# Order of filling products in the last attention's loop, and of the units ahead of it

## The chip, the cores and the metric

One core of a Trainium2 chip runs the whole program. The metric is the device time of one execution in microseconds; lower is better. TensorE (PE) multiplies matrices into PSUM, ScalarE (ACT) and VectorE (DVE) empty PSUM and do the pointwise work, GpSimd (POOL) and SyncE (SP) mostly issue transfers.

## The reference

Two blocks run one after the other on 512 tokens of width 1024. The first is a two-layer transformer; the second, which matters here, is one hybrid layer: a dilated window attention with three groups of heads beside a long convolution, merged by gates. Cut to the attention:

```python
for g, (window, dilation) in enumerate(((128, 1), (512, 4), (2048, 16))):
    radius = window // (2 * dilation)
    o_g, lse_g = dilated_window_attention(qkv[:, :, 0, g], qkv[:, :, 1, g],
                                          qkv[:, :, 2, g], slopes, dilation, radius)
    ...
wts = jax.nn.softmax(jnp.stack(lses, axis=0), axis=0)
o_attn = jnp.einsum('bgsh,gbshe->bshe', wts, jnp.stack(outs, axis=0))
y_attn = o_attn.reshape(B, S, D_ATTN) * jax.nn.silu(g_attn)
```

A softmax over the three groups' own softmaxes equals one softmax over the keys of all three, so the kernel handles each query's 512 + 128 + 128 = 768 scores at once. All is fp32; products of weights are made as three passes over high and low parts.

## The kernel before

**Planner.** The program is written against a scheduler that lays out each engine's instructions from the order in which the code emits them: among instructions whose inputs and buffers are ready in its own model of time, the one emitted first goes first. So the emitted order is a priority. Weight loads and splits stand under a raised priority (AHEAD, 1500 places), so they run ahead. On the chip every engine then takes its instructions strictly in the order laid out.

**Weights.** `unit` brings a block of 1024 x 256 weights in two halves: a transfer on SP into one of three `raw` buffers (L102), a copy to the high part on ACT (L276), the low part on DVE (L277). Two units fit in the weight buffers, so the halves of a further unit are split as the halves of an older one fall free.

**Products.** `mm3` (L282 to L284) issues three matmuls per 128 rows of depth, 24 per product. A queries/keys unit (`queries`, L1287 and on) gives two products of 512 columns, evicted by ACT with 128x512 each: first the queries (L1300, `qT`), then the keys (L1298, `kT`); six products make one pair of heads' three groups. A value unit (`values`) gives four products of 256 columns, evicted by DVE with the bias added (L1256, `v`). `b2_rattn` gives eight products evicted as sigmoids (L1384, `sr`). Each of these is a generator that yields after a product.

**Attention.** `b2_attn` runs four passes, one per pair of heads, with four tasks each (128 queries by 768 keys, for both heads b = 0 and 1). A task has these steps: `scores` (12 matmul instructions, L1338, into the only four-bank buffer `S`); `soft` (per head: DVE adds the distances and takes the extreme, L1346, writing `P`; ACT exponentiates with the sum, L1348; DVE takes the reciprocal, L538, and scales, L542); `prod`, which is `pv_two`: for each head two groups of three 128 x 128 turns (transposes, L516, six per head) into `ptr`, a copy of each group by ACT (L520, `PT`), and at every second task the products with the values (L530, L533) for both; and `after` the fourth task (L1362).

`ptr` and the products of the loop share one ring of three one-bank PSUM buffers (L1325). `P` has three buffers, two of which a task takes (L1345). `pipeline` (L564) emits the tasks one ahead of each other and calls `fill`, which draws a fixed number of products (`steps`, L1367) from the next pass's queries and values; every second of them also draws a step of `stage_weights` (two loads, a scaling on DVE L1227, a split, and two stores L1235), which prepares weights of a later stage. The mix stages call `pipeline` as well, without products to draw.

Ahead of the loop, `run(...)` makes two value units and the first pair's queries and keys with the PSUM pools of the stage before; they are closed at the first pass and the four banks of `S`, one of `ops` and three of the ring take their place.

Of the kernel before, what the change touches and what calls it, by code (L numbers as in the profile page):

```python
# [45 lines left out]
class Net:  # L46
# [138 lines left out]
    def fill(self, n=1):  # L185

        for _ in range(n):
            if self.fillers:
                self.begun = True
                if next(self.fillers[0], "end") == "end":  # L190
                    self.fillers.pop(0)
                    self.begun = False
# [371 lines left out]
    def pipeline(self, tasks, depth, beside=iter(()), steps=(), deep=None):  # L564

        n = len(tasks)  # L570
        ahead = depth

        def fill(m):
            for _ in range(steps[m] if m < len(steps) else 0):
                next(beside, None)
        for t in tasks[:depth]:
            t[0]()
        tasks[0][1]()
        fill(0)
        for m, t in enumerate(tasks):  # L580
            while ahead < n and ahead <= m + (depth if deep is None or m + 1 < deep else depth + 1):
                tasks[ahead][0]()
                ahead += 1
            if m + 1 < n:
                tasks[m + 1][1]()
            t[2]()
            if t[3] is not None:
                t[3]()
            fill(m + 1)
        for _ in beside:  # L590
            pass

# [645 lines left out]
    def b2_attn(self):  # L1238
        nc, tc, a = self.nc, self.tc, self.a
        mm = nc.tensor.matmul  # L1240
        with ExitStack() as es, ExitStack() as rs:
# [4 lines left out]
            def val_bias(g, s):  # L1246
                bv = ap.tile([128, 256], F32, name="bv", tag="bv", bufs=2)
                nc.gpsimd.dma_start(bv, a["b_v_2"][:, 512 * g + 256 * s:512 * g + 256 * s + 256].to_broadcast([128, 256]))
                vals[s].append(ap.tile([128, 4, 256], F32, name="v", tag="v", bufs=4))
                return bv  # L1250

            def value(W, bv, t, s):
                p = self.product()
                for k in range(KB):
                    self.mm3(p[:, :256], [x[:, k, 128 * t:128 * t + 128] for x in self.h2], W[k], k == 0, k == KB - 1)
                nc.vector.tensor_tensor(vals[s][-1][:, t], p[:, :256], bv, OP.add)  # L1256
# [23 lines left out]
            def values(s, g):  # L1280
                W = self.b2_units(2 + 9 * s + g)
                bv = val_bias(g, s)
                for t in range(4):
                    value(W, bv, t, s)
                    yield

            def queries(p_):  # L1287
                qT = ap.tile([128, 3, 512], F32, name="qT", tag="qT", bufs=2)
                kT = ap.tile([128, 3, 512], F32, name="kT", tag="kT", bufs=2)
                qk.append((qT, kT))  # L1290
                for g in range(3):
                    W = self.b2_units(5 + 9 * (p_ // 2) + 3 * (p_ % 2) + g)
                    for b in range(2):
                        p = self.product()
                        for k in range(KB):
                            self.mm3(p, [w[:, 128 * b:128 * b + 128] for w in W[k]], [x[:, k] for x in self.h2], k == 0, k == KB - 1)
                        if b:
                            nc.scalar.activation(kT[:, g], p, AF.Identity, bias=self.bias2(12 + 4 * g + p_))  # L1298
                        else:
                            nc.scalar.activation(qT[:, g], p, AF.Identity, bias=bq[:, g, p_:p_ + 1], scale=scq[:, p_:p_ + 1])  # L1300
                        yield

            def run(*work):
                for _ in chain(*work):
                    pass
# [5 lines left out]
                        next(stage, None)  # L1311
                    yield
            qk, sr = [], []
            run(values(0, 1), values(0, 2), queries(0))
            for s in range(2):
                for pp in range(2):
                    p_ = 2 * s + pp
# [552 lines left out]
```

## Time and profile before

| | |
|---|---|
| Median of 3 runs | 3403.52 us (3399.89 to 3403.88) |
| Profiled execution | 3408.37 us, its span 3406.6 us |
| TensorE busy | 3339.2 us, 98% of the span |
| DVE, ACT, POOL busy | 58%, 32%, 10% |
| Granted TensorE clock, mean | 0.994 |
| Chain that ended last | PE 85%, DVE 5%, issue 5%, DMA 3% |

The span runs from the first to the last instruction of the profiled execution; the rest of its time lies around it. Busy shares are of the span. A matmul's end is modelled: the next one starts well before the end shown (512 columns: 0.39 us shown, 0.23 us from start to start), so rates are read from starts. "Idle before" in a row is the time for which the engine had nothing running, with the instruction that ended the wait.

### The profile page before, as it was taken

To read this page: it belongs to the slowest core of one execution; us is meant where nothing else is said; L and a number is where in the kernel's file an instruction comes from. 1 tells how busy PE (TensorE), PEld (TensorE's weight loads), DVE (VectorE), ACT (ScalarE), POOL (GpSimd) and SP (SyncE) were. 2 spreads that over 40 slices of the span, in tenths; PEclk is the share of its full clock that TensorE was granted. 3 is DMA by queue.
4 is the path that set the end of the run, shared out by engine and by line. 5 is a ranking of instruction groups with operands and counts; after the bars stand their busy time and mean duration, and the time that the engine had idled before them with its cause. 6 is when DMAs were issued, how large, how long until landed. Compare 5 with 4: busy or idle time off the path is not lost.

```text
span 3406.6 us, 50645 instructions
## 1 busy us (share of the span) xinstructions
PE 3339.2 (98%) x20690; PEld 2890.6 (85%) x20690; DVE 1967.3 (58%) x3348; ACT 1097.7 (32%) x1950; POOL 351.1 (10%) x474
## 2 busy tenths in 40 slices
PE   7999999999999999999999999999999999999999
PEld 5888888997698888899888889977888897787877
DVE  6636656756754666666455546576544564444585
ACT  4311112345732121223121123464322244444331
POOL 2300000145000000000000000440000000000051
PEclk8999999999999999999999999999999999999999
DMA  7533334131012444423244441312323225442355
GB/s 261 177 118 118 112 112 130 45 97 41 29 61 81 130 131 130 130 69 100 92 146 154 146 130 41 94 40 80 118 93 99 69 77 168 156 149 96 125 204 213
DMA packets 121513, 388.58 MB, mean 114 GB/s; under 512 B 16791, under 2 KB 26747, under 8 KB 120640
## 3 DMA queue, kind: packets, MB, share of 16 engines
q1 hardware_dynamic: 92672, 311.84, 28.3%
q0 software_dynamic: 28608, 73.50, 7.0%
q8 instruction: 163, 2.67, 0.3%
q14 instruction: 70, 0.57, 0.1%
HBM read 349.91 MB, written 31.89 MB: 112 GB/s over the span
## 4 chain that ended last, share of the span: by engine, by line
PE 85%; DVE 5%; issue 5%; DMA 3%; ACT 1%; POOL 0%; SPq 0%; DVEq 0%; POOLq 0%; ACTq 0%
PE mm L283 23%; PE mm L282 23%; PE mm L284 23%; PE pw L282 3%; PE pw L283 3%; PE pw L284 3%; PE ops L530 2%; PE ptr L516 2%; PE S L611 1%; DMA rawf<-in_w_ada 1%; DVE t L256 0%; DVE wl L277 0%; DVE P L542 0%; PE pad L150 0%; DVE nm L549 0%
## 5 line engine op out<-in xcount | busy, mean ns | idle before, releaser
L282 PE MATMUL mm<-aTh,wh 128*128 128x256 f32 (+1 forms) x2992 | 985.3, 331 | 4.0 <-ACT aTh L259 3.8
L283 PE MATMUL mm<-aTl,wh 128*128 128x256 f32 (+1 forms) x2992 | 987.9, 331 | 0.6 <-DVE aTl L260 0.6
L284 PE MATMUL mm<-aTh,wl 128*128 128x256 f32 (+1 forms) x2992 | 986.6, 330 | 0.0
L282 PEld LDWEIGHTS mm<-aTh,wh 128*128 128x128 f32 x2992 | 569.1, 191 | 58.2 <-ACT aTh L259 4.5
L283 PEld LDWEIGHTS mm<-aTl,wh 128*128 128x128 f32 x2992 | 569.9, 191 | 56.7 <-issue 3.7
L284 PEld LDWEIGHTS mm<-aTh,wl 128*128 128x128 f32 x2992 | 569.9, 191 | 54.0 <-issue 2.9
L277 DVE TENSOR_TENSOR wl<-raw,wh 128x1024 fp32r<-128x1024 f32 x288 | 352.7, 1226 | 299.4 <-ACT wh L276 294.9
L282 PE MATMUL mm<-uh,dh 128*128 128x256 f32 (+1 forms) x1368 | 449.1, 328 | 3.2 <-DVE h L340 1.9
L276 ACT ACTIVATE wh<-raw 128x1024 fp32r<-128x1024 f32 x296 | 313.0, 1059 | 424.7 <-PE mm L283 293.6
L284 PE MATMUL mm<-uh,dl 128*128 128x256 f32 (+1 forms) x1368 | 447.8, 327 | 0.0
L283 PE MATMUL mm<-ul,dh 128*128 128x256 f32 (+1 forms) x1368 | 447.4, 327 | 0.0
L340 DVE SCALAR_TENSOR_TENSOR h<-mm,hg,h 128x256 f32<-128x256 f32 (+1 forms) x512 | 291.5, 581 | 173.6 <-PE mm L284 173.0
L319 DVE TENSOR_TENSOR sil<-sil,mm 128x256 f32<-128x256 f32 (+1 forms) x170 | 90.5, 532 | 343.9 <-PE mm L284 343.6
L282 PEld LDWEIGHTS mm<-uh,dh 128*128 128x128 f32 x1368 | 259.1, 189 | 29.2 <-DVE h L340 2.9
L283 PEld LDWEIGHTS mm<-ul,dh 128*128 128x128 f32 x1368 | 259.0, 189 | 23.8 <-issue 0.8
L284 PEld LDWEIGHTS mm<-uh,dl 128*128 128x128 f32 x1368 | 259.0, 189 | 23.4 <-issue 0.4
L135 DVE SCALAR_TENSOR_TENSOR acc<-rawf,cond,acc 128x1024 f32<-128x1024 f32 x189 | 235.9, 1280 | 68.1 <-DMA rawf<-in_w_ada 67.6
L276 ACT ACTIVATE dh<-rawf 128x1024 fp32r<-128x1024 f32 x88 | 92.0, 1057 | 483.2 <-DMA rawf<-in_ffn_down 372.6
L318 ACT ACTIVATE sil<-mm 128x256 f32<-128x256 f32 (+1 forms) x170 | 79.0, 465 | 461.6 <-PE mm L284 460.3
L277 DVE TENSOR_TENSOR dl<-rawf,dh 128x1024 fp32r<-128x1024 f32 x88 | 107.1, 1223 | 102.2 <-ACT dh L276 102.0
L282 PE MATMUL pw<-aTh,wh 128*128 128x512 f32 x400 | 159.2, 398 | 2.0 <-ACT x L1452 1.1
L283 PE MATMUL pw<-aTl,wh 128*128 128x512 f32 x400 | 156.1, 390 | 0.0
(399 smaller groups left out, 4800.0 us busy)
## 6 DMA issues: line engine op xcount, KB each, us to landing
raw<-in_ffn_up SPq DMA_DIRECT2D x176, 512.0 KB, 3.6
rawf<-in_w_ada SPq DMA_DIRECT2D x168, 512.0 KB, 3.8
raw<-in_w_in SPq DMA_DIRECT2D x100, 512.0 KB, 3.7
rawf<-in_ffn_down SPq DMA_DIRECT2D x88, 512.0 KB, 3.7
raw<-in_w_out SPq DMA_DIRECT2D x24, 512.0 KB, 4.0
wsc<-st POOLq DMA_DIRECT2D x12, 512.0 KB, 2.9
wsc<-raw POOLq DMA_DIRECT2D x12, 512.0 KB, 3.7
Hs<-Hf POOLq DMA_DIRECT2D x16, 256.0 KB, 4.7
```

What stands on the lines that cost most here:

```text
L135: nc.vector.scalar_tensor_tensor(acc[i], raw, self.cond[:, k, x:x + 1], acc[i], op0=OP.mult, op1=OP.add)
L276: self.hi = self.nc.scalar.activation(hi, src, AF.Copy)
L277: return (eng or self.nc.vector).tensor_tensor(lo, src, hi.bitcast(F32), OP.subtract)
L282: mm(ps, w[0], a[0], start=first, stop=False)
L283: mm(ps, w[0], a[1], start=False, stop=False)
L284: mm(ps, w[1], a[0], start=False, stop=last)
L318: nc.scalar.activation(s[:, :n], ps[0][:, :n], AF.Silu)
L319: nc.vector.tensor_tensor(s[:, :n], s[:, :n], ps[1][:, :n], OP.mult)
L340: nc.vector.scalar_tensor_tensor(self.h[:, j, c0:c0 + n], p[:, :n], hg[0][:, j, v:v + 1], self.h[:, j, c0:c0 + n], op0=OP.mult, op1=OP.add)
L516: nc.tensor.transpose(pt[:, 128 * c:128 * c + 128], P[b][:, 128 * (c0 + c):128 * (c0 + c) + 128], self.ident)
L530: nc.tensor.matmul(oo, v(b, c), x.rearrange("p t q -> p (t q)"), start=c == 0, stop=c == n - 1)
L611: self.nc.tensor.matmul(S[:, c:c + n], q, x[:, k], start=i == 0, stop=i == 1)
```

## The change

In `pipeline`, the call that draws the filling products moves up: after the next task's scores and softmax have been emitted, the products now come before this task's turns and value products in place of behind them. In `b2_attn`, the first queries and keys are emitted between the two value units in place of behind both.

```diff
@@ -583,10 +583,10 @@
                 ahead += 1
             if m + 1 < n:
                 tasks[m + 1][1]()
+            fill(m + 1)
             t[2]()
             if t[3] is not None:
                 t[3]()
-            fill(m + 1)
         for _ in beside:
             pass
 
@@ -1311,7 +1311,7 @@
                         next(stage, None)
                     yield
             qk, sr = [], []
-            run(values(0, 1), values(0, 2), queries(0))
+            run(values(0, 1), queries(0), values(0, 2))
             for s in range(2):
                 for pp in range(2):
                     p_ = 2 * s + pp
```

`t[2]` is `prod`, `t[3]` is `after`; `tasks[m + 1][0]` (scores) and `tasks[m + 1][1]` (soft) stand above.

## Rows read from the trace of the kernel before

**Rows 1.** The page, its first part: busy time of each engine.
```profile
PE 3339.2 (98%) x20690; PEld 2890.6 (85%) x20690; DVE 1967.3 (58%) x3348; ACT 1097.7 (32%) x1950; POOL 351.1 (10%) x474
```

**Rows 2.** Table by stretches: us, busy us by engine, clock, DMA share.
```profile
2855.30:3126.80 271.50, 264.68 (x1574) 206.22 (x1572) 125.06 (x199) 136.85 (x215) 13.38 (x25) 1.00 0.41 137
```

**Rows 3.** Waits of PE, 2855.3 to 3126.8: total us, times, longest.
```profile
PE ptr L516 <- DVE P L542: 2.3, 1, 2.3
PE ptr L516 <- ACT sr L1384: 1.5, 2, 0.8
PE S L1338 <- ACT kT L1298: 1.5, 1, 1.5
PE pw L282 <- ACT PT L520: 0.9, 1, 0.9
PE S L1338 <- DVE nm L1346: 0.3, 1, 0.3
...
```

**Rows 4.** Timeline, the first scores: start us, us, engine, line, idle before.
```profile
2855.26 0.39 PE L284 MATMUL mm<-aTh,wl 128*128 128x512 f32 x1
2855.46 1.06 ACT L276 ACTIVATE wh<-raw 128x1024 fp32r<-128x1024 f32 x1 [1.66 <-PE mm L283]
2856.43 0.67 ACT L1298 ACTIVATE kT<-mm,vec 128x512 f32<-128x512 f32 x1
...
2857.15 0.70 PE L1338 MATMUL S<-kT,qT 64*128 64x512 f32 x2 [1.50 <-ACT kT L1298]
```

**Rows 5.** Timeline, first pass: third scores, second task's turns, and DVE meanwhile.
```profile
2878.91 1.57 PE L1338 MATMUL S<-kT,qT 64*128 64x512 f32 x12
2882.77 1.92 PE L516 MATMUL ptr<-ident,P 128*128 128x128 f32 x12 [2.29 <-DVE P L542]
...
2880.67 1.23 DVE L1227 TENSOR_TENSOR raw<-raw,gb 128x1024 f32<-128x1024 f32 x1 [3.64 <-DMA raw<-in_w_out]
```

**Rows 6.** Timeline of PE, last pass: turns directly behind a sigmoid product.
```profile
3117.62 0.39 PE L284 MATMUL pw<-aTh,wl 128*128 128x512 f32 x1
3117.85 0.82 PE L516 MATMUL ptr<-ident,P 128*128 128x128 f32 x6
3119.50 0.93 PE L516 MATMUL ptr<-ident,P 128*128 128x128 f32 x6 [0.84 <-ACT sr L1384]
3120.36 0.65 PE L530 MATMUL ops<-PT,v 128*64 128x256 f32 x2
```

**Rows 7.** Timeline of PE, first pass: turns behind scores, then a product.
```profile
2871.73 1.67 PE L516 MATMUL ptr<-ident,P 128*128 128x128 f32 x12
2873.25 0.50 PE L282 MATMUL pw<-aTh,wh 128*128 128x512 f32 x1
```

**Rows 8.** Timeline, a query product's last column and its eviction.
```profile
3046.88 0.39 PE L284 MATMUL pw<-aTh,wl 128*128 128x512 f32 x1
...
3047.30 0.78 ACT L1300 ACTIVATE qT<-pw,bq,scq 128x512 f32<-128x512 f32 x1 [3.23 <-PE pw L284]
```

**Rows 9.** Timeline, a value unit's last column and its eviction.
```profile
3002.49 0.28 PE L284 MATMUL pw<-wh,aTl 128*128 128x256 f32 x1
...
3003.66 0.42 DVE L1256 TENSOR_TENSOR v<-pw,bv 128x256 f32<-128x256 f32 x1
```

**Rows 10.** Groups by line, 2855 to 3130: busy us, mean ns, idle before.
```profile
L1348 ACT ACTIVATE P<-P,nm 128x768 f32<-128x768 f32 x32 | 29.9, 936 | 7.5 <-DVE nm L1346 7.4
L1346 DVE CUSTOM_DVE_ANT_0 P<-S,dist 128x768 f32<-128x768 f32 x32 | 29.3, 953 | 6.8 <-PE S L1338 6.8
...
L1384 ACT ACT_TABLE_LOAD x5 | 6.4, 1283 | 0.1
```

**Rows 11.** Timeline of PE, the second pass's first scores among the first pass's turns.
```profile
2902.57 1.13 PE L1338 MATMUL S<-kT,qT 64*128 64x512 f32 x4
2903.63 0.88 PE L516 MATMUL ptr<-ident,P 128*128 128x128 f32 x6
...
2906.24 0.50 PE L282 MATMUL pw<-aTh,wh 128*128 128x512 f32 x1
```

## The prediction

> **What bounds the kernel now.** I read the page first. TensorE is busy 98% of the span [rows 1], so only what adds or removes idle time of TensorE can move the end. Other engines matter where TensorE waits for them. Next I read the table by stage for the stretch that the change touches, from the first scores of the last attention to its last product of turned probabilities with values: 271.5 us with 264.68 us busy, at a granted clock of 1.00 [rows 2]. So 6.8 us of visible idle time are to be had there; the reader should keep this ceiling, because 0.2% of the time is 6.8 us as well, and about that is what a measurement of this kernel can tell from no change. Then the waits of TensorE in the stretch [rows 3]: the five longest kinds are 6.5 us together, two of them single long waits. The timeline shows both. At 2855.65 the last column of the first keys ends, and the first scores start only at 2857.15, when ACT has finished the keys' eviction [rows 4]; ACT began that eviction 0.78 us late, because a weight split of 1.06 us, released by the same product, stood before it. At 2880.4 the third scores end and the turns of the second task wait 2.29 us for its probabilities: DVE had queued a multiplication of staged weights before the normalisation, and that waited 3.64 us for its load [rows 5].
>
> **Part A, the filling products moved between the next scores and this task's turns.** No instruction is added or removed. The order in which TensorE gets work of task m goes from scores(m+1), turns(m), product(s) to scores(m+1), product(s), turns(m). The mix stages use the same pipeline without filling products, so nothing moves there. Transfers: each filling product that opens a unit issues two loads of weights on SP, and every second step one staged load on SP and two stores on POOL. They pass only turns(m), which issues no transfer, and their order among themselves and to the softmax steps stays; I cost the moved transfers at nothing, covered by loads that run far ahead (a queue that did bind would look like the 3.64 us of [rows 5]; that is the other end).
>
> What it gains. The 2.3 us wait for probabilities gets a product (24 columns) before it; the probabilities were late by 2.29 us, so the product covers them. The smaller ones (1.5 us in two waits for a sigmoid's eviction, 0.9 and 0.3 us) are collisions of the present order [rows 3]. The four kinds are 5.0 us.
>
> What it costs. Turns go through the same ring of three one-bank buffers as the products (L1325), in four groups of three. Today the scores, about 1.5 us [rows 5], stand between a product and the turns, and in that time ACT empties the product's buffer; the twelve turns then take 1.52 us, 2871.73 to 2873.25 [rows 7]. After the change they follow the product directly. Two groups (0.75 us) find free buffers; the third wants the product's, 0.98 us after the product's last column started (0.23 to its successor plus 0.75). When does that buffer come free?
> - A query product is evicted at once: 1.20 us after the last column's start [rows 8]. The third group waits 0.2 us, and the fourth for the first one's copy, which stands behind the eviction on ACT: some 0.3 us in all (estimate from these rows).
> - A key product is the second of its weight unit, so the weight split stands first: 1.84 us [rows 4]. The same place with a sigmoid product shows what follows, as it is already direct: 3117.85 to 3120.36, 2.51 us in place of 1.52, with 0.84 us marked as waiting for the eviction [rows 6]. That is 1.0; I take 0.9 for keys and 1.0 for sigmoids.
> - A last value of a unit goes out on DVE after 1.59 us [rows 9]: 0.7.
>
> Counting tasks 0 to 2 of the four passes by the product that now precedes their turns (steps in the call of the pipeline): queries 4, keys 4, value 1, sigmoids 3. That is 4 x 0.3 + 4 x 0.9 + 0.7 + 3 x 1.0 = 8.5 us. Bounds for the twelve: from nothing (the planner has other work to put in) to 12 x 1.0. I take 8.5, because I see no such work: the scores after next are not ready (next paragraph), and a further product has no buffer. For task 3 of the first three passes there is work: the next pass's first scores step in, as they do today [rows 11], and I cost it at nothing (0.3 each otherwise).
>
> The second consequence is in the probabilities' ring: three buffers, two per task (L1345). The softmax of task m+1's second head can write only after the first six turns of task m. So it slips behind the product with them, the single scores buffer is released that much later, and the DVE instructions queued behind it are the normalisations. After the first six turns come DVE's 0.95 us [rows 10]; the next scores are then ready some 2.3 us after the product's last column, when the turns end at 2.0 to 2.65. Behind odd tasks the products with values cover it. Behind the four even ones it costs from nothing to 1.2 us each (a weight split of about that length ahead on DVE, 1.23 us in [rows 5] for the like-sized step); I take 0.3, as the next filling columns can go first: 1.2 us.
>
> Third, the tail of the last pass, where no filling product is left between the turns of its tasks 2 and 3. The last softmax waits for the first six turns of task 2, then takes 0.95 us on DVE and 0.94 on ACT [rows 10], and its normalisation, another pass of DVE over the same 768 columns, about a microsecond by the first (estimate); TensorE has 1.5 us of other turns for it. Left over: 0.9 to 2.1 us, the upper end if the sigmoids' table has to be swapped for the exponential's on the path, 1.28 us [rows 10]. I take 1.5 us; 1.0 of it is already lost there today [rows 6], so +0.5.
>
> The Trainium skill ("ScalarE: Activation LUTs", What ACT_TABLE_LOAD costs) prices a switch of table at 1.28 us and a drain of 1.38 us more. The trace agrees with the first number alone: the load takes 1.28 us [rows 10]. By the page the upper end of the tail would be 3.5 us and the sum 1.4 us higher; I stay with the row.
>
> **Part B, the first queries and keys ahead of the third values.** The last product before the first scores becomes a value. If the scores wait only for the keys, the whole 1.5 us goes. But they wait for PSUM as well: the scores' tile takes four banks of the pools just closed, and the same number of products (14) precedes it in either order, so the last one sits in the same buffer. The trace speaks for the bank: in the next pass the first four score columns run at 2902.57, ahead of that pass's last key product, which starts at 2906.24 [rows 11], so they don't need the last keys; yet here the first column waits for the last eviction [rows 4]. A unit's last value is evicted 1.59 us after its last column's start [rows 9], and with half the columns of 0.23 us the next instruction could start 0.12 us after it (estimate); the wait is then 1.47 us, where today's is 1.66 by the same measure (2857.15 less 2855.26 less 0.23). Gain 0.2 us, from 0 to 1.5. Loads of the three weight units change order on SP; each is asked for two units ahead, so nothing (the cover gone: a load, as in [rows 5]).
>
> **The sum.** +8.5 +1.2 +0.5 -5.0 -0.2 = +5.0 us. The profiled execution took 3408.4 us (span 3406.6, 1.8 us outside) and becomes 3413.4; it lies 4.9 us above the median of the runs, which I keep as an offset: 3403.5 + 5.0 = 3408.5 us, 0.15% more.
>
> **Rivals.**
> - Slower: the ring of three binds throughout. Every direct entry costs the 1.0 us of [rows 6], the four even scores wait their 1.2, the tail takes 1.1 more than today, and only the 2.3 and 0.2 us come back: 12 + 4.8 + 1.1 - 2.5 = +15.4, 3418.9 us. It decides from the point where the average entry costs 0.5 us or more with one wait of [rows 5]'s kind left. For it: the one direct entry seen. Against it: half the entries have an early eviction [rows 8]. The Trainium skill ("Perfetto Trace Analysis", Matmuls) asks that independent groups rotate through PSUM banks so that an eviction overlaps the next group; here the overlap given by the scores is what goes, so that rule speaks for this rival.
> - Faster: the emitted order is only a priority, and the planner finds columns for each hole, as it does with the scores in [rows 11]. Then the waits go, all but the bank: -5.0 to -6.5 us, 3397 to 3398.5 us; past 6.8 us only if the spaces around inserted scores close up too. Against: three buffers leave nothing to put in.
> - It does nothing: the planner lays almost the same order, since turns were ready first anyway. 3403.5 us. Against: when both are ready, priority decides.
>
> **Chances.** Forecast 0.50 (3402 to 3412; 0.06 of it beyond 3410.3), slower rival 0.27, faster rival 0.13 (0.08 past the bound, 0.05 within), no effect 0.10. So faster by over 0.2%: 0.08; within: 0.44 + 0.05 + 0.10 = 0.59; slower: 0.06 + 0.27 = 0.33. The range runs from just inside the faster rival to the lower part of the slower one: 3398 to 3416.
>
> **What would show it.** In the changed profile: turns directly behind products, with waits of the second six for ACT's eviction of queries, keys and sigmoids near 0.3 and 0.9 us (A right); their absence with scores or value columns between (faster rival). The 2.3 us wait for probabilities gone. First scores waiting about 1.5 us for DVE's value eviction (B right), or not at all (bank reading wrong). Four waits of scores for the softmax's second head below 0.5 us; at 1 us the slower rival. The forecast is wrong altogether if the stretch's 271.5 us changes by more than 10 us, or if stages outside it move.

## The result, and the profile after

The changed kernel takes 3425.3 us (median, 3424.9 to 3425.6), the kernel before 3403.7 us in the same comparison: 1.0064 times as long, 95% interval 1.0052 to 1.0076. It is slower by 21.6 us, outside the forecast range and some 6 us beyond the slower rival.

The page after, its first part:

```profile
PE 3341.7 (98%) x20690; PEld 2892.6 (85%) x20690; DVE 1968.9 (58%) x3348; ACT 1099.5 (32%) x1950; POOL 351.7 (10%) x474
```

The work is that of [rows 1], but TensorE is "busy" 2.5 us more with the same 20690 instructions, which points at its clock. From here on "the loop" is the stretch from the first scores to the last product with values. In the kernel before it runs from 2857.15 to 3126.87, 269.7 us with 264.4 us busy; behind it come 279.7 us, after the change 279.1. (The profiled execution of before begins the loop 4.8 us later than that of after. In the runs below that leave the part ahead of the loop nearly alone it begins between 2848.8 and 2855.6 us, so most of this is spread between executions.) The table by stretches for the loop after the change (us; busy us of PE, PEld, DVE, ACT, POOL with instructions; clock; DMA share; GB/s):

```profile
2852.37:3144.11 291.74, 270.49 (x1572) 211.69 (x1572) 125.78 (x199) 134.58 (x212) 13.98 (x26) 0.96 0.38 128
```

So the whole loss lies in the loop: +22.0 us, of which TensorE idles 15.9 more (21.2 in place of 5.3) and is busy 6.1 more, at a clock of 0.96 in place of 1.00 [rows 2]. What it waits for there, beside [rows 3] (total us, times, longest):

```profile
PE S L1338 <- DVE nm L1346: 6.6, 2, 5.5
PE ptr L516 <- ACT kT L1298: 5.9, 4, 3.4
PE ptr L516 <- ACT qT L1300: 3.6, 3, 3.1
PE ptr L516 <- ACT sr L1384: 2.7, 3, 0.9
PE ptr L516 <- ACT PT L520: 2.5, 2, 2.2
PE S L1338 <- DVE v L1256: 1.3, 1, 1.3
```

The waits of 2.3 us for probabilities and 0.9 us for `PT` are gone; two of those for sigmoids became three. New are four of over 2 us: 5.52, 3.38, 3.13 and, in the tail, 2.17. The first of them on all engines, from the timeline after (start us, us, engine, line, idle before):

```profile
2872.53 0.82 PE L516 MATMUL ptr<-ident,P 128*128 128x128 f32 x6
2878.87 2.93 PE L1338 MATMUL S<-kT,qT 64*128 64x512 f32 x12 [5.52 <-DVE nm L1346]
2881.73 1.54 PE L516 MATMUL ptr<-ident,P 128*128 128x128 f32 x6
...
2875.98 1.23 DVE L1227 TENSOR_TENSOR raw<-raw,gb 128x1024 f32<-128x1024 f32 x1 [3.72 <-DMA raw<-in_w_out]
...
2877.32 0.62 DVE L542 TENSOR_SCALAR P<-P,rs 128x768 f32<-128x768 f32 x1
2877.85 0.95 DVE L1346 CUSTOM_DVE_ANT_0 P<-S,dist 128x768 f32<-128x768 f32 x1
...
2877.29 1.06 ACT L276 ACTIVATE st<-raw 128x1024 fp32r<-128x1024 f32 x1 [5.37 <-DVE rs L538]
2878.26 0.76 ACT L1300 ACTIVATE qT<-pw,bq,scq 128x512 f32<-128x512 f32 x1
2878.92 0.86 ACT L520 ACTIVATE PT<-ptr 128x384 f32<-128x384 f32 x2
```

DVE stands 3.72 us before a multiplication of staged weights whose load is late, about the length of [rows 5]. Behind it in the queue wait the normalisation and the next extreme (L1346), on which the next scores wait. ACT's next instruction is the split of the same staged weights, so ACT stands 5.37 us; behind it wait the eviction of the queries, whose product ended near 2872.7, and the copies of the first turns. TensorE gets its twelve scores at 2878.87, and they take 2.86 us from start to start in place of 1.51 (2852.37 to 2853.88 in this trace): the clock had fallen.

The clock in four microseconds around the end of each of three waits (columns as above):

```profile
2876.37:2880.37 4.00, 1.50 (x4) 0.84 (x6) 3.54 (x6) 3.08 (x5) 0.66 (x2) 0.56 0.58 204
...
2948.37:2952.37 4.00, 3.48 (x10) 1.94 (x12) 3.18 (x6) 3.01 (x7) 0.07 (x1) 0.52 0.99 301
...
3132.37:3136.37 4.00, 2.60 (x11) 2.03 (x11) 0.78 (x2) 3.47 (x8) 0.00 (x0) 0.56 0.39 131
```

0.52 to 0.56 of full speed is close to the lower of the two levels (1.2 of 2.4 GHz, 0.5). The three waits are those of 5.52, 3.38 and 2.17 us. Shared among three drops, the 6.1 us of longer busy time are about 2 us each. That share is an estimate: two loops below at a clock of 1.00 also differ by 2.8 us in busy time (e8 and e9), so not all of the 6.1 us need be the clock.

### The profile page after: what moved, and what is told of

Read it like the earlier page. It is cut to its first block, busy times and chain, and to the rows that moved or that the text cites. A ratio compares the mean times of both kernels' runs of the same rounds, so it can differ in the third digit from the quotient of the medians.

```text
span 3423.2 us, 50639 instructions
## 1 busy us (share of the span) xinstructions
PE 3341.7 (98%) x20690; PEld 2892.6 (85%) x20690; DVE 1968.9 (58%) x3348; ACT 1099.5 (32%) x1950; POOL 351.7 (10%) x474
## 4 chain that ended last, share of the span: by engine, by line
PE 84%; issue 7%; DVE 5%; DMA 2%; ACT 1%; POOL 0%; SPq 0%; DVEq 0%; POOLq 0%; ACTq 0%
PE mm L283 23%; PE mm L282 23%; PE mm L284 23%; PE pw L282 2%; PE pw L283 2%; PE pw L284 2%; PE ops L530 2%; PE ptr L516 2%; PE S L611 1%; DVE t L256 0%; DVE wl L277 0%; PE pad L150 0%; DMA rawf<-in_w_ada 0%; PE ops L499 0%; DVE nm L549 0%
## 5 line engine op out<-in xcount | busy, mean ns | idle before, releaser
L276 ACT ACTIVATE wh<-raw 128x1024 fp32r<-128x1024 f32 x296 | 312.9, 1059 | 433.7 <-PE mm L283 293.2
```

What stands on the lines that cost most here:

```text
L276: self.hi = self.nc.scalar.activation(hi, src, AF.Copy)
```

## Experiments

The loop's length is from one profiled execution of each kernel; four kernels that leave it nearly alone (before, and three below) lie between 269.1 and 270.9 us, so read it to about 1 us. Where work was moved out of the loop the whole time doesn't tell the loop's price, and the loop's length is compared.

| kernel | loop us | PE busy | clock | median us (before beside it) | ratio, 95% |
|---|---|---|---|---|---|
| before | 269.7 | 264.4 | 1.00 | | |
| after | 291.7 | 270.5 | 0.96 | 3425.3 (3403.7) | 1.0052 to 1.0076 |
| e1 part A alone | 293.2 | 270.4 | 0.97 | 3425.3 (3404.4) | 1.0048 to 1.0078 |
| e2 part B alone | 269.2 | 264.5 | 1.00 | 3404.6 (3404.4) | 0.9990 to 1.0009 |
| e10 B, pools turned round | 270.9 | 265.5 | 0.99 | 3403.4 (3404.6) | 0.9987 to 1.0006 |
| e7 after, staging behind the loop | 272.6 | 262.6 | 0.99 | 3471.4 (3404.6) | 1.0186 to 1.0218 |
| e8 before, staging behind the loop | 261.7 | 260.6 | 1.00 | 3471.3 (3404.6) | 1.0180 to 1.0210 |
| e3 after, staging on GpSimd | 282.9 | 269.2 | 0.98 | 3417.1 (3404.4) | 1.0023 to 1.0053 |
| e4 before, staging on GpSimd | 273.1 | 266.6 | 0.99 | 3407.6 (3404.4) | 0.9999 to 1.0018 |
| e9 e7 and four P buffers | 260.4 | 257.8 | 1.00 | 3466.4 (3404.6) | 1.0163 to 1.0194 |
| e12 after, four P buffers | 273.7 | 262.9 | 0.99 | 3408.5 (3404.4) | 1.0007 to 1.0024 |
| e13 before, four P buffers | 269.1 | 264.5 | 1.00 | 3403.9 (3404.4) | 0.9991 to 1.0009 |
| e16 after, staging behind the turns | 295.8 | 271.5 | 0.96 | 3433.6 (3404.2) | 1.0071 to 1.0101 |
| e17 before, staging ahead of the turns | 283.2 | 268.9 | 0.98 | 3417.3 (3404.2) | 1.0025 to 1.0054 |
| e18 e12, staging behind the turns | 276.5 | 264.2 | 0.98 | 3409.6 (3404.2) | 1.0002 to 1.0021 |
| e19 e18, pools turned round | 276.0 | 264.2 | 0.99 | 3408.0 (3404.2) | 1.0005 to 1.0024 |
| e22 after, staging with a buffer of its own | 293.1 | 268.9 | 0.98 | 3427.9 (3404.8) | 1.0057 to 1.0085 |
| e23 before, the same | 277.8 | 268.9 | 0.98 | 3412.8 (3404.8) | 1.0018 to 1.0036 |
| e14 before, 7 staged steps ahead of the loop | 274.9 | 265.7 | 0.98 | 3430.4 (3404.4) | 1.0061 to 1.0086 |
| e15 e14 with both parts, pools and four P | 275.7 | 265.5 | 0.98 | 3422.5 (3404.4) | 1.0042 to 1.0067 |

### Which part: e1 and e2

```diff
# e1, against the kernel after
-            run(values(0, 1), queries(0), values(0, 2))
+            run(values(0, 1), values(0, 2), queries(0))
# e2, against the kernel before: the reverse
```

> Part A alone (the filling products before the turns), the units ahead of the loop in the old order. If the loop's order is the whole cause: 3424 to 3426 us, as with both parts. If the order of the units ahead of the loop takes part: less by what it costs, so anything below 3421 us speaks for it.

> Part B alone (first queries and keys ahead of the third values), the loop in the old order. By the reading that the first scores wait for a PSUM bank whose last tenant is evicted late in either order: 3403 to 3404 us, within 0.5 us of before. If only the keys were waited for: 1.5 us less, 3402.

Part A alone has the whole loss, part B alone nothing that can be measured. B's one wait is as forecast: with both parts the first scores wait 1.31 us for DVE's eviction of the value (`v`, L1256) where they waited 1.50 for ACT's of the keys [rows 4], and 1.30 us with part B alone.

### The bank behind part B: e10

```diff
# e10: e2, and the loop's pools opened in the opposite order
-  sps = self.pool(es, "b2s", 1, space=PSUM)
-  po = self.pool(es, "b2po", 1, space=PSUM)
   self.pa = self.pm = self.pool(es, "b2ps", 3, space=PSUM)
+  po = self.pool(es, "b2po", 1, space=PSUM)
+  sps = self.pool(es, "b2s", 1, space=PSUM)
```

> Part B alone, with the loop's three PSUM pools opened in the opposite order, so that the scores' four banks are no longer the last product's. Bank reading: the first scores wait for nothing (1.3 to 1.5 us less than part B alone, 3402 to 3403.3 us where part B alone gave 3404.6). If the wait has another reason it stays, within 0.3 us of part B alone.

The scores' tile now takes banks of products long evicted. The timeline of e10, the last value column and the first scores:

```profile
2850.63 0.28 PE L284 MATMUL mm<-wh,aTl 128*128 128x256 f32 x1
2850.84 1.57 PE L1338 MATMUL S<-kT,qT 64*128 64x512 f32 x12
```

No wait is left, so it was the bank: scores need neither the last value nor, after B, the last keys. The whole time doesn't show the 1.3 us.

### Staged steps out of the loop: e7 and e8

```diff
-  self.pipeline(tasks, 1, staging(beside), ...)
+  self.pipeline(tasks, 1, beside, ...)      # run(stage) behind the loop makes all twelve
```

> Both parts, with the staged weights of the later stage worked behind the loop in place of in it; the loop's products, scores, turns and softmax are the same. Queue theory: without staged steps no engine of the loop stands behind their transfers, so of the loop's 291.7 us (first scores to last product with values) about 12 to 15 go, to 277 to 280 us, the granted clock of the loop rises from 0.97 to 0.99 or more, and the only wait of turns over 2 us is in the last pass's tail. Ring theory: 285 us or more, with long waits still spread over the passes. The whole time also holds what staging costs behind the loop, so the loop's length decides, not the time.

> The kernel before with the staged weights worked behind the loop: the control for the run above. Queue theory: the loop of 269.7 us loses the wait of 2.3 us and little else, 266 to 268 us. The whole time tells what staging costs behind the loop: 3401 us if it is covered there, more if the later products wait for it. The difference of the loops of the two runs is the price of the order without staging: by the forecast's terms 8.5 + 1.2 + 0.5 us, about 10; by the queue theory 8 to 12.

The loops of the two orders, after (e7) and before (e8), by the table by stretches:

```profile
2853.27:3125.84 272.57, 262.64 (x1560) 206.16 (x1560) 101.79 (x178) 118.84 (x196) 1.62 (x3) 0.99 0.18 60
```

```profile
2852.32:3113.97 261.65, 260.55 (x1560) 204.11 (x1560) 99.49 (x178) 120.00 (x197) 0.74 (x2) 1.00 0.19 60
```

Without staged steps the new order costs 10.9 us (272.6 less 261.7). The staged steps cost the old order 8.1 us (269.7 less 261.7) and the new one 19.2 (291.7 less 272.6). The loss of 22.0 us is therefore 10.9 for the order and 11.1 for staged steps that became more exposed; by the columns of the table 7.1 of the 11.1 are idle time of TensorE and 4.0 longer busy time. Both loops are shorter than expected (277 to 280 and 266 to 268 us); their difference lies within the expected 8 to 12, and the one wait of turns over 2 us is in the last pass's tail, as the queue theory had it. The whole times don't show the loops' difference: behind the loop TensorE stands once for a weight split on ACT, 57.6 us in e7 and 70.8 in e8, so what follows the loop takes 342 and 356 us in place of some 280.

### Staged steps on another engine: e3 and e4

```diff
-  nc.vector.tensor_tensor(r3, r3, gb..., OP.mult)
+  nc.gpsimd.tensor_tensor(r3, r3, gb..., OP.mult)
-  self.split(*w, raw)
+  nc.gpsimd.tensor_copy(w[0], raw)
+  nc.gpsimd.tensor_tensor(w[1], raw, w[0].bitcast(F32), OP.subtract)
```

> Both parts, but the staged weights (scaling, high and low part) are worked by GpSimd in place of DVE and ACT; their transfers and the order of everything else stay. Queue theory (the new order exposes ACT and DVE instructions that stand behind staged weights waiting for a transfer; three such places in the loop, some 5.5 + 1.3, 3.4 + 2.2 + 1.4 and 3.1 us of TensorE's waits): about 14 us back, 3409 to 3413 us, and no wait over 2 us of scores or turns in the loop. Ring theory (the turns directly behind a product wait for its buffer whatever else is queued): little back, 3422 to 3425 us, with the long waits still there.

> The kernel before with the staged weights worked by GpSimd. Queue theory: its one wait of 2.3 us for probabilities goes, and some of the smaller ones: 3400 to 3401.5 us. Ring theory: the same as before, 3403 to 3404. Against both: if GpSimd is too slow for the staging and holds its buffers longer, weights arrive late and it is slower than 3404.

Neither theory's range was met: 3417.1 us lies between the two for e3, with waits of 3.95 and 2.56 us left in the passes, and e4 is slower than before, the branch that stood against both. With nothing staged in the queues of ACT and DVE the new order gets 8.9 us of its loop back, fewer than the 11.1 to 19.2 that were to be had, and the old order loses 3.4. One reason is in the trace of e3:

```profile
2881.46 3.33 DVE L277 TENSOR_TENSOR wl<-raw,wh 128x1024 fp32r<-128x1024 f32 x1 [4.04 <-ACT wh L276]
...
2880.22 1.03 POOL L1233 CAST st<-raw 128x1024 fp32r<-128x1024 f32 x1
2881.33 2.39 POOL L1234 TENSOR_TENSOR raw<-raw,st 128x1024 fp32r<-128x1024 f32 x1
```

The same weight split takes DVE 1.23 us on its own. Behind this one stand the next extreme, its exponential on ACT and the eviction of keys, for which TensorE waits 3.95 us. GpSimd's subtraction ended at 2883.72, and DVE's split 1.07 us later, as if it had begun only then. The Trainium skill ("SBUF — State Buffer", Who interferes with whom) states that a DVE operation on two tensors in SBUF and a GpSimd operation that reads SBUF contend for one port pair, and that the later one is blocked until the other ends; this row agrees.

### A fourth buffer for the probabilities: e9, e12 and e13

```diff
-  P = bp.tile([128, 768], F32, name="P", tag="P", bufs=3)
+  P = bp.tile([128, 768], F32, name="P", tag="P", bufs=4)
# room for it, e12 and e13: two sigmoids less in buffers of their own
-  room = ... for i in range(2)
+  room = ... for i in range(3)
-  tag="sr", bufs=4) if u < 2 else room[2 * u + b - 4]
+  tag="sr", bufs=2) if u < 1 else room[2 * u + b - 2]
# e9 takes the room from the staged weights, which it opens behind the loop as in e7
```

> As the first of this call, and with four buffers for probabilities in place of three (room comes from the staged weights' buffers, which are taken later). The second head's softmax no longer waits for the turns before. If the forecast's reading of that ring is right, the tail's wait of 2.2 us and the waits of scores for the softmax (1.1 us) go and the scores no longer stand between the turns' groups: the loop is 3 to 5 us shorter than with three. If the ring of probabilities matters not: within 1 us.

> Both parts, staged weights in the loop as in the change, and four buffers for probabilities in place of three (room comes from the sigmoids' tiles, of which two more go into the old queries' and keys' buffers). If the ring of probabilities is the cause, because it keeps the next scores from standing between turns and from covering ACT and DVE: the loop of 291.7 us falls to 268 to 274 us and the time to 3402 to 3408 us, with no wait over 3 us and the granted clock of the loop at 0.99 or more. If the staged weights' queueing is a cause of its own that the order exposes either way: 278 to 284 us, 3412 to 3418 us.

> The kernel before with four buffers for probabilities: the control. In the old order the scores stand ahead of the turns anyway, so by either theory nothing: loop 268 to 271 us, 3402 to 3406 us. A gain over 3 us would say that the ring of three costs the old order too.

Turns behind a query product in e9, by the timeline of PE:

```profile
2875.31 0.82 PE L516 MATMUL ptr<-ident,P 128*128 128x128 f32 x6
2876.06 1.57 PE L1337 MATMUL S<-kT,qT 64*128 64x512 f32 x12
2877.56 0.88 PE L516 MATMUL ptr<-ident,P 128*128 128x128 f32 x6
```

With a fourth buffer the softmax of the next task needn't wait for these turns, so the scores after next are ready, and the planner lays them between the two halves: 1.50 us of work, in which ACT empties the product. The order's 10.9 us are gone (260.4 against 261.7), far more than the 3 to 5 us expected. With the staged steps in the loop, 18.0 of the 22.0 us are gone (e12, 273.7, within its range; its 3408.5 us are just outside, and still slower than the kernel before). The same buffer gives the old order nothing (e13, 269.1), as expected, since there the scores stand in that place anyway. The Trainium skill ("Perfetto Trace Analysis", Optimization Strategy) reads the same gap, repeated on the engine that should be busy, as a possible sign of too few buffers; these runs agree for the order's own gaps. What stays in e12 are above all waits for evictions and copies behind staged steps on ACT (the longest three follow splits ahead of which ACT stood 3.6, 5.6 and 4.5 us):

```profile
PE ptr L516 <- ACT PT L520: 4.1, 2, 3.3
PE ptr L516 <- ACT kT L1298: 4.0, 4, 1.4
PE ptr L516 <- ACT qT L1300: 1.9, 1, 1.9
```

### The place of the staged steps: e16 to e19

```diff
# e16 against after; e18 the same with four P buffers; e19 that with e10's pools
             fill(m + 1)          # products only
             t[2]()
             if t[3] is not None:
                 t[3]()
+            put(m + 1)           # the staged steps that these products drew
# e17 against before: put(m + 1) ahead of t[2](), fill(m + 1) stays behind
```

> The changed kernel, but the staged steps are emitted behind the task's turns, as before the change; the products stay ahead of the turns. Theory, the place: with the staged steps behind the loop the changed order takes 272.6 us in the loop, and in the old order staged steps cost 8.1 us (269.7 less 261.65); if the other 11.1 us come from staged steps standing ahead of the turns' copies on ACT and DVE, the loop takes some 281 us (278 to 283) and the time is 3414 to 3415 us. Rival, the tight order: without scores between product and turns any staged step hits TensorE wherever it is emitted; the loop stays at 289 to 293 us and the time at 3423 to 3426.

> The kernel before, with only the staged steps emitted ahead of the turns; products and units as before. Theory, the place: the staged steps then hold ACT and DVE ahead of the turns' copies and the normalisation, and the loop goes from 269.7 to some 278 to 283 us, the time to 3412 to 3417. Rival, the tight order: with scores between product and turns the staged steps stay covered, the loop at 268 to 272 us and the time within 3 us of the kernel before.

> The change with four buffers for the probabilities and the staged steps behind the turns. Theory, the place: of the 13.3 us that staged steps cost the loop with four buffers (273.7 less 260.4), 5 us come from the place; the loop takes some 268.5 us and the time is 3402 to 3404.5 us. Rival, the tight order: as with the staged steps ahead, 273 to 275 us and 3407 to 3410 us.

> As the third of these, with the loop's PSUM pools opened in the opposite order, so that the first scores don't wait for the last value's bank. Theory, the place: 1 to 1.5 us less than the third, 3401 to 3403.5 us, the same as the kernel before or up to 0.1% less. Rival, the tight order: 3406 to 3409 us.

The change had moved the staged steps ahead of the turns together with the products, and I took that for the cause. It fell from one side: emitted behind the turns again, they cost the new order as much or more (e16, 295.8 us, slower than even the rival had it), with four buffers too (e18 and e19, 276.5 and 276.0 us beside e12's 273.7). The timeline of e16 shows why, ACT first and then PE:

```profile
2944.72 1.06 ACT L276 ACTIVATE st<-raw 128x1024 fp32r<-128x1024 f32 x1 [6.86 <-DMA wsc<-st]
...
2951.27 1.06 ACT L276 ACTIVATE st<-raw 128x1024 fp32r<-128x1024 f32 x1 [3.90 <-DMA wsc<-st]
2952.23 1.04 ACT L276 ACTIVATE wh<-raw 128x1024 fp32r<-128x1024 f32 x1
2953.18 0.67 ACT L1305 ACTIVATE kT<-pw,vec 128x512 f32<-128x512 f32 x1
...
2946.16 0.89 PE L516 MATMUL ptr<-ident,P 128*128 128x128 f32 x6
2953.90 1.33 PE L516 MATMUL ptr<-ident,P 128*128 128x128 f32 x5 [6.85 <-ACT kT L1305]
```

Two staged splits still stand ahead of an eviction of keys, and the second waits 3.90 us until the store of the first has left the one buffer `st`. The emitted place doesn't decide what stands behind a staged step. From the other side it does count: in e17 the old order loses 13.5 us, just above the theory's range. In its longest wait DVE runs three staged multiplications in a row ahead of the softmax:

```profile
2918.97 3.49 DVE L1234 TENSOR_TENSOR raw<-raw,gb 128x1024 f32<-128x1024 f32 x3
...
2925.46 2.93 PE L1345 MATMUL S<-kT,qT 64*128 64x512 f32 x12 [4.88 <-DVE nm L1353]
```

### A load buffer for staged steps alone: e22 and e23

```diff
# both against the kernel named, with the sigmoids' room of e12, P at three buffers
-  raw = self.raw()
+  raw = bp.tile([128, 1024], F32, name="raws", tag="raws", bufs=1)
```

> The changed kernel, the staged steps load into a buffer of their own in place of the ring of three that they share with the weight units (room for it from the sigmoids' buffers; the probabilities keep three). Theory, late loads: in the changed kernel every long hold of ACT or DVE was a staged step waiting for a load that the ring had let start late; with a buffer of its own the load is there before the step, the holds go, and the loop takes 272.6 us, as with the staged steps behind it, to 277; 3407 to 3411 us. Rival, in-order queues under any staging: one buffer makes the next load wait for the last store, the holds stay 3 us and longer; the loop 286 to 296 us, 3420 to 3428 us.

> The kernel before with the same buffer of its own. Theory, late loads: the 2.3 us wait for the probabilities goes and most of the 8.1 us that staged steps cost the loop with it; the loop takes 262 to 266 us, 3396 to 3400.5 us. Rival: 268 to 272 us, 3402 to 3406 us.

The theory was wrong on both sides. The rival's ranges hold for e22; e23 is slower than they allow (277.8 us, 3412.8). With one buffer the next load waits for the last store to leave it, and in e22 DVE waits 2.8 to 6.2 us ahead of all but one staged multiplication behind the first. From e22's timeline, one of them, and ACT behind it:

```profile
2946.05 1.23 DVE L1227 TENSOR_TENSOR raws<-raws,gb 128x1024 f32<-128x1024 f32 x1 [5.41 <-DMA raws<-in_w_out]
...
2947.36 1.06 ACT L276 ACTIVATE st<-raws 128x1024 fp32r<-128x1024 f32 x1 [4.17 <-DVE raws L1227]
2948.33 1.99 ACT L276 ACTIVATE wh<-raw 128x1024 fp32r<-128x1024 f32 x2
2950.22 0.67 ACT L1298 ACTIVATE kT<-pw,vec 128x512 f32<-128x512 f32 x1
```

So this tests a buffer of its own only together with a depth of one; two were not tried.

### Staged steps ahead of the loop: e14 and e15

```diff
# e14 against before; e15 the same with part A, part B, e10's pools and e12's buffers
-  run(values(0, 1), values(0, 2), queries(0))
+  run(staging(chain(values(0, 1), values(0, 2), queries(0))))
```

> The kernel before with seven of the twelve staged steps drawn by the fourteen products ahead of the loop, which have five PSUM buffers and no softmax beside them, and five left in the loop. If what staging costs the loop (8.1 us, by the run without it) goes with the steps: the loop falls to 263 to 267 us; ahead of it nothing is lost as TensorE idles there only for the first scores; 3398 to 3402 us. If the transfers bind instead (staged loads and stores beside those of the units): the same time is lost ahead of the loop, 3403 us or more.

> The changed kernel with all three remedies: four buffers for probabilities, seven staged steps ahead of the loop, the loop's PSUM pools in the opposite order. By the runs so far: without staging and with four buffers its loop took 260.4 us, 1.2 less than the old order's; with five steps left some 263 to 266 us, no wait before the first scores; 3395 to 3400 us, faster than the kernel before. If the new order has a cost that these do not reach: 3403 us or more.

Both gains failed to come; the other branch, 3403 us or more, is what happened. Ahead of the loop TensorE now waits for its own weights, which share the ring of three with the staged loads (waits of PE in e14, 2780 us to the first scores):

```profile
PE mm L282 <- ACT wh L276: 11.8, 3, 8.8
```

The same list of the kernel before, from 2780 us on, is empty up to the one wait of [rows 4]. The loop doesn't gain either: 274.9 us, with five staged steps left in it.

## Why the prediction was wrong

By its own mark (the stretch of 271.5 us changed by more than 10) the forecast is wrong altogether.

**What was right.** Nothing moved outside the loop. The reason that no work fills the holes: three buffers for the probabilities; e9 shows it from the other side. Part B and its bank: 1.46 us by the forecast's measure (2852.37 less 2850.79 less 0.12) for 1.47. The waits that were to go: 2.3 and 0.9 us are gone.

**The sum without staged steps came out nearly, through errors that cancel.** It had +8.5, +1.2 and +0.5 us, 10.2 in all; e7 less e8 is 10.9. By the entries of e7: turns behind queries wait 0.21 us (0.3 forecast), as here in the trace after, beside [rows 7]:

```profile
2902.09 0.82 PE L516 MATMUL ptr<-ident,P 128*128 128x128 f32 x6
2903.12 0.93 PE L516 MATMUL ptr<-ident,P 128*128 128x128 f32 x6 [0.21 <-ACT qT L1300]
2903.88 0.50 PE L282 MATMUL pw<-aTh,wh 128*128 128x512 f32 x1
```

Behind keys 0.84 to 0.89 (0.9), behind the value 0.65 (0.7), behind sigmoids 0.89 at the first and 0.12 at the other two (1.0). Where scores or other work step in, as they do behind two of the keys, nothing; so all entries of turns are 5.2 us for 8.5, 0.84 of it at a fourth task that was costed at nothing. The scores' waits for the softmax are 2.1 us, two of 1.06 (1.2 forecast). The tail waits 2.60 us (1.5 taken, 2.1 the upper bound), with the table load on the path; in the trace after it waits 2.17. A further 2.1 us are longer busy time of TensorE, with one drop of its clock in it, of which the forecast said nothing. The 5.0 us of gains were counted too high by the sigmoids' 1.5, which the direct entries keep: they are 2.7 us now. The 0.84 us of [rows 6] were even taken off twice, once in these 1.5 and once in the tail's +0.5 (1.5 less 1.0).

**The step that failed** is "I cost the moved transfers at nothing, covered by loads that run far ahead". It looked at transfers as queues of SP and POOL. What binds are the staged *instructions* that stand in line on DVE and ACT, each waiting for a load or store of 3 to 4 us (median 4.3 and 3.2 to 3.8 us to landing on the page after). The view for it was there: the groups by line of the loop's ACT, first before and then after the change (busy us, mean ns, idle us before):

```profile
L276 ACT ACTIVATE st<-raw 128x1024 fp32r<-128x1024 f32 x12 | 12.7, 1060 | 38.3 <-DVE raw L1227 17.6 <-DMA raw<-in_w_proj 16.0 <-issue 4.4
```

```profile
L276 ACT ACTIVATE st<-raw 128x1024 fp32r<-128x1024 f32 x12 | 12.7, 1058 | 29.3 <-DMA raw<-in_w_proj 13.9 <-DVE rs L538 9.5 <-issue 3.1
```

Before the change ACT already stood 38.3 us ahead of twelve staged splits, more than after it. The forecast's other premise, that a query product "is evicted at once", was read from [rows 8] alone; of the nine query evictions in the loop before, three stood behind a staged split and one behind a softmax, and began 1.12 to 4.35 us after their product's last column had started, in place of 0.43. The twelfth staged split shows what changed, first before and then after:

```profile
3026.61 1.06 ACT L276 ACTIVATE st<-raw 128x1024 fp32r<-128x1024 f32 x1 [3.95 <-DMA raw<-in_w_proj]
3027.57 0.76 ACT L1300 ACTIVATE qT<-pw,bq,scq 128x512 f32<-128x512 f32 x1
...
3028.39 0.93 PE L516 MATMUL ptr<-ident,P 128*128 128x128 f32 x6 [0.22 <-ACT qT L1300]
```

```profile
3033.43 1.06 ACT L276 ACTIVATE st<-raw 128x1024 fp32r<-128x1024 f32 x1 [5.03 <-DMA raw<-in_w_proj]
3034.39 0.76 ACT L1300 ACTIVATE qT<-pw,bq,scq 128x512 f32<-128x512 f32 x1
...
3035.21 0.93 PE L516 MATMUL ptr<-ident,P 128*128 128x128 f32 x6 [3.13 <-ACT qT L1300]
```

ACT waits for the same staged load with a query eviction behind it, and TensorE loses 0.22 us before the change and 3.13 after. Before it, 1.5 us of scores lay between the product and the turns. The change didn't lengthen these holds in total; it put TensorE's next need of ACT right behind the product's end, some 0.75 us later (two groups of turns), and so into them. The wait of 3.38 us ends behind a staged split too (ACT stood 4.14 us ahead of it), that of 5.52 us behind a staged multiplication on DVE (3.72 us, shown above). The 8.1 us of staged cost became 19.2. The range's other end for this, one wait of 3.64 us [rows 5], counted one hold where three fell in the path. (A staged step has one load, not two as the kernel's description says, and eight of the twelve have the scaling on DVE.)

**The second omission is the clock.** Three of the longer waits came with a stretch near half speed each, and the loop was busy 6.1 us longer, which no list of waits shows. The slower rival (+15.4) had no staged steps and no clock; with its entries at 1.0 us it was too dear by itself, and still 6 us short.

**What stays open.** Why the planner lays a staged split ahead of an eviction that is due earlier on the chip; that its model takes loads and stores to be shorter than the traces show would explain it, and was not tested. How the 11.1 us divide among single holds, and how much of the 4.0 us of busy time in them is the clock, isn't separated. No kernel here beats the one before by more than the measurement can tell (e10 and e13 come nearest).

## What to carry to other kernels

Ask of a reorder not only which instructions move but how soon the bound engine will need the next one on each in-order queue, and list what already stands waiting in that queue; holds that cost nothing behind cover cost their full length without it. Check the depth of the buffer ring that would have to supply substitute work: here one buffer more took back 18 of the loop's 22 us. Read a cost such as an eviction's delay from all its instances, not from one row. And price a long wait of TensorE with the clock that may fall with it.

## What the runs showed of the hardware

- The granted clock didn't fall after every wait of TensorE. In the kernel before it stayed at 1.00 behind the 2.29 us of [rows 5]; after the change it stayed so behind a wait of 3.13 us that ended at 3035.21, and fell to 0.56 around one of 2.17 us in the tail, shortly after another of 0.89. In e7 it fell to 0.58 behind 2.60 us in the tail. The length of the one wait doesn't tell. The loop with one drop (e7) was busy 2.1 us longer than the one beside it (e8), the loop with three (after) 6.1 us longer.
- GpSimd and DVE got in each other's way: a DVE subtraction of 128x1024 took 3.33 us beside one of 2.39 us on GpSimd (e3), in place of 1.23.
